# A hybrid RWKV-7 and Mamba-2 layer: gram results and chain outputs kept twice, block matrices in 64 columns, values and normed outputs transposed on TensorE

## The chip, the cores and the metric

The kernel runs on one core of a Trainium2 chip. The metric is the device time of one execution in microseconds (us). Before the change the median of three runs is 2758.5 us (2756.22 to 2762.81). On a difference of less than about 0.2% (5.5 us) a measurement of this kernel can't tell a change from none.

## What is computed

One inference step of a single layer over 592 rows (16 meta rows, 512 prompt rows, 64 rows of a running stream), model width 2048, all in float32. The part that matters here is the RWKV-7 mixer: 16 heads of width 64, a state matrix per head, and for every time step

```
def step(S, inp):
    r_t, w_t, k_t, v_t, kk_t, ka_t = inp
    sa = jnp.einsum('bhij,bhj->bhi', S, kk_t)
    S = S * w_t[:, :, None, :] - sa[..., None] * ka_t[:, :, None, :] + v_t[..., None] * k_t[:, :, None, :]
    return S, jnp.einsum('bhij,bhj->bhi', S, r_t)
```

Its output is normed over each head (mean and variance of 64 values), scaled and shifted by `lnx_w` and `lnx_b`; a bonus term `sum(r*k*r_k)*v` is added, and the sum is multiplied by a gate. The rest of the layer: a norm and a combined input projection ahead of the mixers, a Mamba-2 mixer beside RWKV, the output projection, a gated feed-forward net, a last norm.

## The kernel before

The whole layer is one instruction stream per engine. TensorE (PE) does the big products with float32 split into a high and a low part (three fp32r matmuls for one). These products are the main stream: input tiles `k0 r0 k1 r1 v0 k2 r2 ...` of the projection (96 matmuls of 296 columns each; `k`, `r`, `v` of eight head pairs, four `z` tiles in between), then the Mamba tiles `B C x`, the rest of `z`, the output projection (`mwo`) and the feed-forward net (`a x r y`). All else is written as generators (`go(...)`, line 206) that put their instructions into the gaps of the main stream. The order on each engine is fixed when the program is built, by a planner with a cost table (`tick` and `Timed`, lines 136 to 185): `beat` (215) looks, between groups of main matmuls, which generators are due by these costs, and lets them emit up to their next `yield`. On the chip each engine then runs its list strictly in order. Nearly every instruction of the kernel is recorded under line 159, the line of the wrapper, so groups are told apart by tile names and shapes.

RWKV runs per head pair j (two heads in the two halves of the 128 partitions), 640 padded time steps as 10 chunks of 64. Per pair:

- `shift_k`, `shift_r`, `shift_v` (708 to 723) take the projected tiles out of PSUM, `decay` and `pre_k` (725, 743) make decays and keys. `shift_v(j)` needs `vd` of pair j-1, `shift_r(j)` needs `rk` of j-1.
- `pre_r` (789) builds `KB` and `ST`, then waits at line 810 until the three `px` products of pair j-1 are emitted, and then issues 20 gram matmuls (tile `gr`, contraction over 64 partitions) in six groups. `gram_out` (770) takes each group out: masked halves to `ST` and `GB` on VectorE (DVE), blocks of the triangular system to `NX` and `NS` on ScalarE (ACT).
- Then `V.transpose(NN, NX)` (line 830), again after `px` of j-1 because `NN` shares memory with `YB`, and the triangular solve: 31 steps of two GpSimd (POOL) instructions (832 to 837).
- `steps` (855) transposes `KB` on PE (tile `tr`). `solved` (880) lays the solution out as block matrices `Zd` (two 64x64 blocks in 128 columns), makes `pm` from `NS`, and `MB` from it. `applied` (918) makes `pb = Zd^T GB` (mark `py`) and `px = MB^T pb`, ten 128x128 matmuls each, and `PT` from them.
- `values` (959) lays the values out in time order: eight DVE transposes in blocks of 32x32 into `V0`, after `cl` (chain finished) of pair j-1.
- `chain` (984) runs the ten chunks one after the other (tile `p`, two matmuls, evictions on ACT and DVE, two matmuls, a state update per chunk) and writes `Y`. It waits for the mark `chain` of j-1, which `post` of j-1 sets after it has read `Y` for the last time.
- `post` (1034) norms `Y`, transposes it back with eight DVE transposes into `yb` (mark `chain`, 1061), loads the gate into `rs` and applies `lnx_w`, `lnx_b`, bonus and gate; two DMAs write the result out.

For 64-row by 64-row work the profile's `gr` form reads 64*128 (rows x columns of the array); every other of these matmuls has the whole array, 128*128. A plain float32 matmul is two `MATMUL` records, a PE transpose one. Four PSUM banks serve the main stream, three go round among all these tasks (`get`, `put`), one is the chain's.

Of the kernel before, what the change touches and what calls it, by code (L numbers as in the profile page):

```python
# [11 lines left out]
F32R = mybir.dt.float32r  # L12
# [5 lines left out]
P = 128  # L18
# [68 lines left out]
def tile_hybrid(ctx, tc, xt, wq, wg, wd, lrw, cst, vec, s0w, s0m, y_out, sh_out, wkv_out, cv_out, sm_out):  # L87
# [61 lines left out]
    class Timed:  # L149
# [5 lines left out]
        def __getattr__(self, op):  # L155
            f, e = getattr(self.eng, op), self.e

            def call(out, *a, **k):
                r = f(out, *a, **k)  # L159
                part = 0.1 * (out.shape[0] <= 64)  # L160
                if e == "PE":
                    n = out.free_size()
                    tick(e, n / 2400 + 0.0133 if a[1].dtype == F32R else 0.175 if op == "transpose" else max(0.218, 0.15 + n / 1100))
                else:
# [37 lines left out]
    def load(dst, src):  # L202
        SY.dma_start(dst, src)
        cur[0].t = max(cur[0].t, now() + 2.5)
# [466 lines left out]
    pos_zv = pos[0]  # L671
    R, ses, MVs, st_o = {}, [], [], []
    hrow = [slice(0, 64), slice(64, 128)]
    vrow = [slice(64, 128), slice(0, 64)]

    def A2():

        lrp.close()
        al2, p2 = arena(a2p.enter_context(tc.tile_pool(name="a2p", bufs=1)).tile([P, A2W], F32, name="mem2"), A2W)
        R["al2"], R["pos2"] = al2, p2  # L680
        R["KB"] = al2(1280, NC, P)
        R["GB"] = al2(1280, NC, P)
        R["NS"] = al2(640, 5, P)
        R["NX"] = al2(1024, 32, 32)
# [12 lines left out]
        R["XX"] = al2(388)  # L697
        st_o.extend(al2(64) for _ in range(2))
        G.memset(R["NX"], 0.0)
        G.memset(R["NS"], 0.0)  # L700
        G.memset(R["Zd"], 0.0)
        unit()
        G.tensor_scalar(R["MB"], cc("idn").unsqueeze(1).broadcast_to([P, NC, P]), 1.0, None, ALU.mult)
        for h in range(2):
            G.memset(PT[h][vrow[h], :, vrow[h]], 0.0)
# [64 lines left out]
    def gram_out(j, h, c0, n, b, pg):  # L770

        yield "VA"
        gb_, st, kx = R["GB"], R["ST"][j % 2][h], 64 * h
        q, m = vrow[h], cc("m3")[:, 64 - 64 * h:192 - 64 * h]
# [6 lines left out]
        A.copy(R["NX"][hi, c0:c0 + n, :], pg[hi, 0:n, hi])  # L781
        A.copy(R["NS"][lo, c0 // 2:(c0 + n) // 2, hi], pg[lo, 0:n:2, hi])
        A.copy(R["NS"][hi, c0 // 2:(c0 + n) // 2, lo], pg[lo, 1:n:2, hi])
        put(b)
# [4 lines left out]
    def pre_r(j):  # L789
# [65 lines left out]
    def steps(j):  # L855
# [4 lines left out]
        for c0, n in groups:  # L860
# [7 lines left out]
            for h in range(2):  # L868
                A.copy(R["GB"][hrow[h], c0:c0 + n, hrow[h]], pg[hrow[h], 0:n, hrow[h]])
            for h in range(2):  # L870
# [9 lines left out]
    def solved(j):  # L880
# [16 lines left out]
        for c in range(5):  # L897
            PE.matmul(pm[:, c, :], R["NS"][:, c, :], R["ZM"][:, c], start=True, stop=True)
        aside()
        for q in range(4):  # L900
            d = slice(32 * q, 32 * q + 32)
            for e, i0, i1, g in ((V, 0, 10, 3), (V, 10, 11, 2)):
                e.tensor_copy(R["Zd"][d, :, 32 * q + 3 * i0:32 * q + 3 * i0 + g * (i1 - i0)].rearrange("p c (i g) -> p c i g", g=g),
                              Zc[d, i0:i1, 0:10 * g].rearrange("p i (g c) -> p c i g", g=g))
        cur[0].aside = False
        yield "A"
        for h in range(2):
            lo, hi = slice(64 * h, 64 * h + 32), slice(64 * h + 32, 64 * h + 64)
            for par, q in enumerate((hi, lo)):
                A.activation(R["MB"][hi, par::2, lo], pm[q, :, 0:32], AF.Copy, scale=-1.0)  # L910
        put(b)
# [6 lines left out]
    def applied(j, g, c0, n):  # L918
# [24 lines left out]
    def bonus(j):  # L943
# [90 lines left out]
    def post(j):  # L1034

        Y, MV, bon = c3(R["Y"]), MVs[0], bons[j % 2]
        yield from until(("post", j - 1), then="V")
# [6 lines left out]
        yield "A"  # L1044
        A.activation(yb, R["Y"], AF.Square)
        yield "V"
# [5 lines left out]
        V.tensor_tensor(Y, Y, bc(MV[:, NC:2 * NC]), ALU.mult)  # L1052
        yield "V"
        for w in range(2):
            for h in range(2):
                for t in range(2):
                    q = vrow[h].start + 32 * t
                    V.transpose(c3(yb)[64 * h + 32 * w:64 * h + 32 * w + 32, :, 32 * t:32 * t + 32],
                                Y[q:q + 32, :, 32 * w:32 * w + 32])
                yield "V"  # L1060
# [6 lines left out]
        yield "V"  # L1067
        V.tensor_tensor(yb, yb, rs, ALU.mult)
        SY.dma_start(YAD[j][:, 0:NS], yb[:, 0:NS])
# [4 lines left out]
    for g in range(3):  # L1074
        mark(("py", -1, g))
        mark(("px", -1, g))
    for q in ("rk", "chain", "pb", "pre", "prek", "post", "kb", "T", "vd", "Tm", "cl"):
        for i in (-1, -2):
            mark((q, i))
# [1085 lines left out]
```

## Time and profile before

| | |
|---|---|
| runs (three) | 2756.22, 2758.5, 2762.81 us |
| profiled execution, its own time | 2759.71 us |
| its span, first to last instruction | 2757.6 us |
| mean granted TensorE clock | 0.974 |
| PE busy | 2646.3 us (96%) |
| DVE busy | 2187.0 us (79%) |
| ACT busy | 1405.1 us (51%) |
| POOL busy | 385.9 us (14%) |

Each engine's busy time is set against the span; a busy PE can still run at half clock, so a row's granted clock is read with it (1.00 is 2.4 GHz, 0.50 is 1.2 GHz). The idle time ahead of an instruction is told in brackets with what ended it. The RWKV stage, from the first gram matmul at about 155 us to the last chain step at about 840 us, is where the change acts; after it PE is nearly always busy.

### The profile page before, as it was taken

What the parts mean: (1) busy time and instruction counts of PE and PEld (TensorE: products, weight loads), DVE (VectorE), ACT (ScalarE), POOL (GpSimd) and SP (SyncE); (2) the same over time, 40 slices, a digit from 0 to 9 for tenths busy, and PEclk for the clock granted to TensorE, in tenths of its full rate; (3) what the DMA queues carried; (4) which work ended last, traced back from release to release, by engine and by line L of the source; (5) the groups of instructions that cost most, each with busy time, mean ns of one, the idle gap of its engine ahead of it and who ended that gap; (6) DMA issues with size and microseconds to landing.
All of it is one profiled execution on the core that took longest, in us unless ns stands there. A gap on an engine that the chain in (4) does not pass through costs nothing.

```text
span 2757.6 us, 51938 instructions
## 1 busy us (share of the span) xinstructions
PE 2646.3 (96%) x19236; PEld 2580.2 (94%) x19236; DVE 2187.0 (79%) x4216; ACT 1405.1 (51%) x3013; POOL 385.9 (14%) x673
## 2 busy tenths in 40 slices
PE   8998899989999999999999999999999989999997
PEld 7888789988998989999999999999999989999997
DVE  7675787878878675568898888889888868888885
ACT  5645565656555453454454444545444434444544
POOL 3224334443401120120000000000000000000004
PEclk9999799999999999999999999999999999999999
DMA  5421121222222344343344444444344385654623
GB/s 182 171 71 54 52 71 58 67 62 74 61 88 86 92 145 132 114 146 122 124 159 132 151 133 142 144 146 145 131 152 130 123 275 194 218 186 156 203 71 108
DMA packets 196461, 349.57 MB, mean 127 GB/s; under 512 B 26096, under 2 KB 102000, under 8 KB 196080
## 3 DMA queue, kind: packets, MB, share of 16 engines
q1 hardware_dynamic: 196208, 346.26, 39.0%
q8 instruction: 151, 2.47, 0.4%
q14 instruction: 102, 0.84, 0.1%
HBM read 281.13 MB, written 65.06 MB: 126 GB/s over the span
## 4 chain that ended last, share of the span: by engine, by line
PE 79%; DVE 5%; ACT 5%; POOL 3%; issue 2%; DMA 2%; DVEq 0%; SPq 0%; ACTq 0%; POOLq 0%
PE y L159 15%; PE a L159 14%; PE r L159 14%; PE x L159 7%; PE mwo L159 7%; DVE mem L159 4%; POOL mem L159 3%; PE mx L159 3%; ACT mem L159 3%; PE mv L159 3%; PE mk L159 2%; PE mr L159 2%; PE mz L159 2%; PE p L159 2%; PE me L159 2%
## 5 line engine op out<-in xcount | busy, mean ns | idle before, releaser
L159 ACT CAST memr<-mem 128x512 fp32r<-128x512 f32 (+2 forms) x1230 | 714.1, 586 | 900.2 <-PE y L159 208.2
L159 DVE TENSOR_TENSOR memr<-mem,memr 128x512 fp32r<-128x512 f32 (+2 forms) x1076 | 691.8, 648 | 262.0 <-ACT memr L159 257.4
L159 DVE TENSOR_TENSOR mem<-mem 128x576 f32<-128x576 f32 (+9 forms) x1016 | 696.9, 702 | 21.7 <-DMA mem<-x1d 10.8
L159 POOL TENSOR_TENSOR mem<-mem 128x84 f32<-128x84 f32 (+28 forms) x583 | 337.0, 579 | 2218.8 <-ACT mem L159 1553.8
L159 ACT ACTIVATE mem<-mem 64x64 f32<-64x64 f32 (+12 forms) x413 | 217.1, 534 | 174.6 <-DVE mem L159 155.1
L159 PE MATMUL y<-memr 128*128 128x288 f32 x1352 | 206.6, 300 | 15.3 <-DVE mem L159 15.3
L159 PE MATMUL mwo<-memr 128*128 128x288 f32 x1536 | 210.4, 298 | 0.0
L159 PEld LDWEIGHTS mwo<-memr 128*128 128x128 f32 x1536 | 205.9, 189 | 3.0 <-issue 2.5
L159 PEld LDWEIGHTS y<-memr 128*128 128x128 f32 x1352 | 192.2, 192 | 15.9 <-issue 15.9
L159 PE MATMUL r<-ffm,memr 128*128 128x288 f32 x1348 | 202.7, 297 | 1.6 <-DMA ffm<-pd 1.1
L159 PE MATMUL x<-memr 128*128 128x288 f32 x1352 | 201.4, 295 | 0.0
L159 PE MATMUL y<-ffm,memr 128*128 128x288 f32 x1356 | 201.2, 295 | 0.2
L159 PE MATMUL a<-memr 128*128 128x288 f32 x1352 | 199.7, 294 | 1.2 <-DVE memr L159 1.2
L159 PE MATMUL r<-memr 128*128 128x288 f32 x1352 | 199.1, 294 | 0.0
L159 PE MATMUL a<-ffm,memr 128*128 128x288 f32 x1328 | 197.1, 295 | 0.0
L159 PEld LDWEIGHTS r<-ffm,memr 128*128 128x128 f32 x1348 | 188.3, 190 | 2.8 <-ACT ffm L159 1.3
L159 PEld LDWEIGHTS y<-ffm,memr 128*128 128x128 f32 x1356 | 187.7, 188 | 0.7 <-DMA ffm<-pd 0.4
L159 PEld LDWEIGHTS a<-memr 128*128 128x128 f32 x1352 | 186.9, 188 | 1.4 <-DVE memr L159 1.4
L159 PEld LDWEIGHTS x<-memr 128*128 128x128 f32 x1352 | 187.8, 188 | 0.0
L159 PEld LDWEIGHTS r<-memr 128*128 128x128 f32 x1352 | 186.2, 188 | 0.0
L159 PEld LDWEIGHTS a<-ffm,memr 128*128 128x128 f32 x1328 | 183.9, 188 | 0.0
L159 PE MATMUL mk<-memr 128*128 128x296 f32 x768 | 125.3, 313 | 4.6 <-DVE mem L159 4.6
(184 smaller groups left out, 4051.6 us busy)
## 6 DMA issues: line engine op xcount, KB each, us to landing
mem<-in_wg SPq DMA_DIRECT2D x176, 512.0 KB, 3.4
mem<-in_wq SPq DMA_DIRECT2D x268, 256.0 KB, 2.7
mem<-in_wd SPq DMA_DIRECT2D x128, 320.0 KB, 3.3
pd<-mem SPq DMA_DIRECT2D x280, 144.0 KB, 2.0
memr<-pd SPq DMA_DIRECT2D x80, 288.0 KB, 6.3
ffm<-pd SPq DMA_DIRECT2D x60, 288.0 KB, 6.6
mem<-lrd SPq DMA_DIRECT2D x16, 320.0 KB, 3.8
mem<-in_xt SPq DMA_DIRECT2D x16, 296.0 KB, 5.7
```

Source lines behind the costliest of these rows:

```text
L159: r = f(out, *a, **k)
```

## The change

Six things, in the order of the diff:

1. The planner's table prices a matmul whose stationary operand has 64 rows at 0.6 of what it had (grams too).
2. `GB`, `NS` and `Y` exist twice, by the parity of j; the second `Y` lies in `rs`. `Zd`, `MB` and `NS` have 64 columns, each half of the partitions holding its own 64x64 block.
3. `pm`, `pb` and `px` are two matmuls of 64x64 blocks each instead of one of 128x128.
4. The grams of pair j wait for the `NN` transpose of j-1 and the `pb` products of j-2, instead of the `px` products of j-1. The chain of j waits for `chain` of j-2 and `cl` of j-1.
5. `values` and `post` transpose on PE (helper `turn`: nine transposes of 128 columns, one half one, and one small matmul that turns chunk 0 into the other half), and evict with ACT copies (values, seven) or with DVE `tensor_scalar` (post, seven), which also apply `lnx_w` and `lnx_b`.
6. The gate is loaded into `bon`, after the bonus was added, instead of into `rs`.

```diff
-  tick(e, ... else max(0.218, 0.15 + n / 1100))
+  tick(e, ... else max(0.218, 0.15 + n / 1100) * (0.6 if a[0].shape[0] == 64 else 1))
...
-        R["GB"] = al2(1280, NC, P)
-        R["NS"] = al2(640, 5, P)
+        R["GB"] = [al2(1280, NC, P)]
+        R["NS"] = [al2(320, 5, 64) for _ in range(2)]
...
-        R["Y"] = al2(TR)
+        Ys.extend((al2(TR), rs))
...
-        R["Zd"], R["MB"] = al2(1280, NC, P), al2(1280, NC, P)
+        R["GB"].append(al2(1280, NC, P))
+        R["Zd"], R["MB"] = al2(640, NC, 64), al2(640, NC, 64)
...
-        yield from until(*[("px", j - 1, g) for g in range(3)], then="P")
+        yield from until(("nt", j - 1), *[("py", j - 2, g) for g in range(3)], then="P")
...
         V.transpose(NN, NX.rearrange("p c t -> p t c"))
+        mark(("nt", j))
...
-            PE.matmul(pm[:, c, :], R["NS"][:, c, :], R["ZM"][:, c], start=True, stop=True)
+            for q in hrow:
+                PE.matmul(pm[q, c, :], R["NS"][j % 2][q, c, :], R["ZM"][q, c], start=True, stop=True)
...
-            PE.matmul(pg[:, c - c0, :], R["Zd"][:, c, :], R["GB"][:, c, :], start=True, stop=True)
+            for q in hrow:
+                PE.matmul(pg[q, c - c0, :], R["Zd"][q, c, :], R["GB"][j % 2][q, c, :], start=True, stop=True)
...
-            PE.matmul(pg[:, c - c0, :], R["MB"][:, c, :], yb_[:, c - c0, :], start=True, stop=True)
+            for q in hrow:
+                PE.matmul(pg[q, c - c0, :], R["MB"][q, c, :], yb_[q, c - c0, :], start=True, stop=True)
...
+    def turn(dst, a, c):
+        if c < NC - 1:
+            PE.transpose(dst, a[:, CH * c:CH * c + 2 * CH], cc("idn"))
+        else:
+            PE.transpose(dst[0:64], a[:, CH * c:], cc("idn"))
+            q = hrow[0]
+            PE.matmul(dst[64:128, 0:64], a[q, 0:CH], cc("idn")[q, q], start=True, stop=True)
...
-        for w in range(2):
-            for h in range(2):
-                for t in range(2):
-                    q = vrow[h].start + 32 * t
-                    V.transpose(V0[q:q + 32, h, :, 32 * w:32 * w + 32],
-                                c3(zv)[64 * h + 32 * w:64 * h + 32 * w + 32, :, 32 * t:32 * t + 32])
-                yield "V"
+        for c0, n in groups:
+            yield "P"
+            b = yield from get()
+            pv = bank(b, f"vt{j}{c0}").rearrange("p (c x) -> p c x", x=P)
+            for c in range(c0, c0 + n):
+                turn(pv[:, c - c0, :], zv, c)
+            yield "A"
+            A.copy(V0[vrow[1], 1, c0:c0 + n, :], pv[vrow[1], 0:n, hrow[1]])
+            m = min(n, NC - 1 - c0)
+            A.copy(V0[vrow[0], 0, c0 + 1:c0 + 1 + m, :], pv[vrow[0], 0:m, hrow[0]])
+            if m < n:
+                A.copy(V0[vrow[0], 0, 0, :], pv[vrow[0], m, hrow[0]])
+            put(b)
...
-        yield from until(("chain", j - 1), ("pb", j), ("v", j), ("T", j))
-        EC, st, Y = ECs[j % 3], R["ST"][j % 2], c3(R["Y"])
+        yield from until(("chain", j - 2), ("cl", j - 1), ("pb", j), ("v", j), ("T", j))
+        EC, st, Y = ECs[j % 3], R["ST"][j % 2], c3(Ys[j % 2])
...
+            V.tensor_scalar(c3(yb)[hrow[0], c0:c0 + n, :], pv[hrow[0], 0:n, vrow[0]], *ab_(0), ALU.mult, ALU.add)
+            V.tensor_scalar(c3(yb)[hrow[1], c0 + 1:c0 + 1 + m, :], pv[hrow[1], 0:m, vrow[1]], *ab_(1), ALU.mult, ALU.add)
+            if m < n:
+                V.tensor_scalar(c3(yb)[hrow[1], 0, :], pv[hrow[1], m, vrow[1]], *ab_(1), ALU.mult, ALU.add)
...
-        load(rs, LRD[j, 2][:, 0:TR])
-        V.tensor_scalar(yb, yb, vv("lw", j), vv("lb", j), ALU.mult, ALU.add)
+        V.tensor_tensor(yb, yb, bon, ALU.add)
+        load(bon, LRD[j, 2][:, 0:TR])
         yield "V"
-        V.tensor_tensor(yb, yb, bon, ALU.add)
-        yield "V"
-        V.tensor_tensor(yb, yb, rs, ALU.mult)
+        V.tensor_tensor(yb, yb, bon, ALU.mult)
```

In `post` the eight DVE transposes give way to three groups of `turn` as in `values`, evicted by the `tensor_scalar` lines shown.

## Rows read from the trace of the kernel before

**Rows 1.** The page: span, and part 1 (busy time by engine).

```profile
span 2757.6 us, 51938 instructions
PE 2646.3 (96%) x19236; PEld 2580.2 (94%) x19236; DVE 2187.0 (79%) x4216; ACT 1405.1 (51%) x3013; POOL 385.9 (14%) x673
```

**Rows 2.** Stretches of the RWKV stage: us, busy PE, PEld, DVE, ACT, POOL, PEclk, DMA, GB/s.

```profile
155.00:240.00 85.00, 71.22 (x454) 66.98 (x453) 56.52 (x99) 40.51 (x98) 33.01 (x64) 0.88 0.22 69
...
300.00:346.00 46.00, 37.83 (x184) 31.96 (x183) 36.57 (x75) 30.93 (x82) 5.99 (x18) 0.65 0.14 47
...
405.00:420.00 15.00, 10.11 (x45) 7.71 (x45) 11.87 (x25) 11.12 (x37) 1.17 (x3) 0.66 0.22 74
...
490.00:500.00 10.00, 8.08 (x48) 7.03 (x47) 7.74 (x17) 6.61 (x21) 0.00 (x0) 0.83 0.33 87
...
563.00:582.00 19.00, 11.88 (x58) 10.15 (x58) 11.80 (x30) 14.19 (x43) 0.00 (x0) 0.64 0.20 66
...
sum 685.00, PE 636.85 PEld 597.83 DVE 525.52 ACT 403.18 POOL 239.00; mean PE 63.68 PEld 59.78 DVE 52.55 ACT 40.32 POOL 23.90
```

**Rows 3.** The same view for three stretches at half clock.

```profile
315.00:346.00 31.00, 26.12 (x94) 20.77 (x95) 22.01 (x45) 21.19 (x61) 5.24 (x16) 0.50 0.04 11
409.50:419.00 9.50, 6.19 (x25) 4.80 (x25) 7.43 (x16) 6.28 (x25) 0.32 (x1) 0.51 0.10 35
568.50:581.50 13.00, 8.98 (x38) 7.66 (x39) 8.76 (x22) 8.33 (x33) 0.00 (x0) 0.54 0.08 26
```

**Rows 4.** POOL's timeline (start, us, instruction): the second solve and the third.

```profile
267.82 31.15 POOL L159 TENSOR_TENSOR mem<-mem 128x31 f32<-128x31 f32 x62 [35.20 <-DVE mem L159]
...
339.58 32.54 POOL L159 TENSOR_TENSOR mem<-mem 128x31 f32<-128x31 f32 x62 [38.40 <-DVE mem L159]
```

**Rows 5.** PE's timeline between these solves (start, us, instruction [idle <-releaser]).

```profile
304.45 1.20 PE L159 MATMUL pm<-mem 128*128 128x33 f32 x10
...
313.77 0.85 PE L159 MATMUL px<-mem 128*128 128x128 f32 x4 [3.04 <-ACT mem L159]
314.87 4.24 PE L159 MATMUL gr<-mem 64*128 64x128 f32 x16 [0.25 <-ACT mem L159]
```

**Rows 6.** DVE's groups from 300 to 326 us (busy us, mean ns | idle).

```profile
L159 DVE STREAM_TRANSPOSE mem<-mem 32x320 f32<-32x320 f32 x14 | 7.0, 503 | 0.3
```

**Rows 7.** Groups by form, 100 to 1000 us (busy us, mean ns | idle before).

```profile
L159 DVE STREAM_TRANSPOSE mem<-mem 32x320 f32<-32x320 f32 x128 | 64.0, 500 | 2.5
...
L159 ACT COPY mem<-tr 64x256 f32<-64x256 f32 x64 | 22.3, 368 | 8.1 <-PE tr L159 5.5 <-DMA yad<-mem 1.9
...
L159 DVE TENSOR_TENSOR mem<-gr,mem 64x256 f32<-64x256 f32 x48 | 20.3, 422 | 3.4 <-PE gr L159 2.7
...
L159 PE MATMUL tr<-mem,mem 128*128 128x128 f32 x80 | 15.4, 317 | 0.0
...
L159 DVE TENSOR_SCALAR mem<-mem 128x640 f32<-128x640 f32 x16 | 9.3, 582 | 0.2
```

**Rows 8.** PE's timeline in a stretch without stalls, and at one burst of transposes.

```profile
459.75 2.16 PE L159 MATMUL mr<-memr 128*128 128x296 f32 x14
461.79 2.05 PE L159 MATMUL pb<-mem 128*128 128x128 f32 x16
463.60 0.78 PE L159 MATMUL mr<-memr 128*128 128x296 f32 x4
...
469.71 1.16 PE L159 MATMUL gr<-mem 64*128 64x128 f32 x8
470.80 0.54 PE L159 MATMUL mr<-memr 128*128 128x296 f32 x2
...
494.52 0.60 PE L159 MATMUL tr<-mem,mem 128*128 128x128 f32 x4
494.87 1.13 PE L159 MATMUL mv<-memr 128*128 128x296 f32 x4
```

**Rows 9.** DMA issues: tiles, queue, count, KB each, median us to landing.

```profile
mem<-lrd SPq DMA_DIRECT2D x16, 320.0 KB, 3.8
```

More of the change, by code (lines that the diff above doesn't have):

```diff
@@ L162, in call @@
                     n = out.free_size()
-                    tick(e, n / 2400 + 0.0133 if a[1].dtype == F32R else 0.175 if op == "transpose" else max(0.218, 0.15 + n / 1100))
+                    tick(e, n / 2400 + 0.0133 if a[1].dtype == F32R else 0.175 if op == "transpose" else max(0.218, 0.15 + n / 1100) * (0.6 if a[0].shape[0] == 64 else 1))
                 else:
@@ L671, in tile_hybrid @@
     pos_zv = pos[0]
-    R, ses, MVs, st_o = {}, [], [], []
+    R, ses, MVs, st_o, Ys = {}, [], [], [], []
     hrow = [slice(0, 64), slice(64, 128)]
@@ L699, in A2 @@
         G.memset(R["NX"], 0.0)
-        G.memset(R["NS"], 0.0)
+        for q in R["NS"]:
+            G.memset(q, 0.0)
         G.memset(R["Zd"], 0.0)
         unit()
-        G.tensor_scalar(R["MB"], cc("idn").unsqueeze(1).broadcast_to([P, NC, P]), 1.0, None, ALU.mult)
+        for q in hrow:
+            G.tensor_scalar(R["MB"][q], cc("idn")[q, q].unsqueeze(1).broadcast_to([64, NC, 64]), 1.0, None, ALU.mult)
         for h in range(2):
@@ L772, in gram_out @@
         yield "VA"
-        gb_, st, kx = R["GB"], R["ST"][j % 2][h], 64 * h
+        gb_, ns_, st, kx = R["GB"][j % 2], R["NS"][j % 2], R["ST"][j % 2][h], 64 * h
         q, m = vrow[h], cc("m3")[:, 64 - 64 * h:192 - 64 * h]
@@ L781, in gram_out @@
         A.copy(R["NX"][hi, c0:c0 + n, :], pg[hi, 0:n, hi])
-        A.copy(R["NS"][lo, c0 // 2:(c0 + n) // 2, hi], pg[lo, 0:n:2, hi])
-        A.copy(R["NS"][hi, c0 // 2:(c0 + n) // 2, lo], pg[lo, 1:n:2, hi])
+        A.copy(ns_[lo, c0 // 2:(c0 + n) // 2, 32:64], pg[lo, 0:n:2, hi])
+        A.copy(ns_[hi, c0 // 2:(c0 + n) // 2, 0:32], pg[lo, 1:n:2, hi])
         put(b)
@@ L868, in steps @@
             for h in range(2):
-                A.copy(R["GB"][hrow[h], c0:c0 + n, hrow[h]], pg[hrow[h], 0:n, hrow[h]])
+                A.copy(R["GB"][j % 2][hrow[h], c0:c0 + n, hrow[h]], pg[hrow[h], 0:n, hrow[h]])
             for h in range(2):
@@ L902, in solved @@
             for e, i0, i1, g in ((V, 0, 10, 3), (V, 10, 11, 2)):
-                e.tensor_copy(R["Zd"][d, :, 32 * q + 3 * i0:32 * q + 3 * i0 + g * (i1 - i0)].rearrange("p c (i g) -> p c i g", g=g),
+                e.tensor_copy(R["Zd"][d, :, 32 * (q % 2) + 3 * i0:32 * (q % 2) + 3 * i0 + g * (i1 - i0)].rearrange("p c (i g) -> p c i g", g=g),
                               Zc[d, i0:i1, 0:10 * g].rearrange("p i (g c) -> p c i g", g=g))
@@ L909, in solved @@
             for par, q in enumerate((hi, lo)):
-                A.activation(R["MB"][hi, par::2, lo], pm[q, :, 0:32], AF.Copy, scale=-1.0)
+                A.activation(R["MB"][hi, par::2, 0:32], pm[q, :, 0:32], AF.Copy, scale=-1.0)
         put(b)
@@ L933, in applied @@
         for c in range(c0, c0 + n):
-            PE.matmul(pg[:, c - c0, :], R["MB"][:, c, :], yb_[:, c - c0, :], start=True, stop=True)
+            for q in hrow:
+                PE.matmul(pg[q, c - c0, :], R["MB"][q, c, :], yb_[q, c - c0, :], start=True, stop=True)
         mark(("px", j, g))
@@ L1034, in post @@
     def post(j):
-        Y, MV, bon = c3(R["Y"]), MVs[0], bons[j % 2]
+        Y, MV, bon = c3(Ys[j % 2]), MVs[0], bons[j % 2]
         yield from until(("post", j - 1), then="V")
@@ L1044, in post @@
         yield "A"
-        A.activation(yb, R["Y"], AF.Square)
+        A.activation(yb, Ys[j % 2], AF.Square)
         yield "V"
@@ L1052, in post @@
         V.tensor_tensor(Y, Y, bc(MV[:, NC:2 * NC]), ALU.mult)
-        yield "V"
[L1054 to L1060, printed above, removed]
+        for c0, n in groups:
+            yield "P"
+            b = yield from get()
+            pv = bank(b, f"yt{j}{c0}").rearrange("p (c x) -> p c x", x=P)
+            for c in range(c0, c0 + n):
+                turn(pv[:, c - c0, :], Ys[j % 2], c)
+            yield "V"
+            m = min(n, NC - 1 - c0)
+            ab_ = lambda h: (VE[hrow[h], _VOFF["lw"][0] + j:_VOFF["lw"][0] + j + 1], VE[hrow[h], _VOFF["lb"][0] + j:_VOFF["lb"][0] + j + 1])
+            V.tensor_scalar(c3(yb)[hrow[0], c0:c0 + n, :], pv[hrow[0], 0:n, vrow[0]], *ab_(0), ALU.mult, ALU.add)
+            V.tensor_scalar(c3(yb)[hrow[1], c0 + 1:c0 + 1 + m, :], pv[hrow[1], 0:m, vrow[1]], *ab_(1), ALU.mult, ALU.add)
+            if m < n:
+                V.tensor_scalar(c3(yb)[hrow[1], 0, :], pv[hrow[1], m, vrow[1]], *ab_(1), ALU.mult, ALU.add)
+            put(b)
         mark(("chain", j))
         yield from until(("vd", j), then="V")
-        load(rs, LRD[j, 2][:, 0:TR])
-        V.tensor_scalar(yb, yb, vv("lw", j), vv("lb", j), ALU.mult, ALU.add)
+        V.tensor_tensor(yb, yb, bon, ALU.add)
+        load(bon, LRD[j, 2][:, 0:TR])
         yield "V"
-        V.tensor_tensor(yb, yb, bon, ALU.add)
-        yield "V"
-        V.tensor_tensor(yb, yb, rs, ALU.mult)
+        V.tensor_tensor(yb, yb, bon, ALU.mult)
         SY.dma_start(YAD[j][:, 0:NS], yb[:, 0:NS])
@@ L1075, in tile_hybrid @@
         mark(("py", -1, g))
+        mark(("py", -2, g))
         mark(("px", -1, g))
-    for q in ("rk", "chain", "pb", "pre", "prek", "post", "kb", "T", "vd", "Tm", "cl"):
+    for q in ("rk", "chain", "pb", "pre", "prek", "post", "kb", "T", "vd", "Tm", "cl", "nt"):
         for i in (-1, -2):
```

## The prediction

> **What bounds the kernel now.** I read the page first: PE is busy for 2646 of the 2757.6 us of the span, DVE for 2187 [rows 1]. The kernel is bound by PE, so a change can only win where PE stands still or runs at half clock, and it pays for every PE instruction that it adds. Then the stretches of the RWKV stage, 155 to 840 us [rows 2]: of 685 us PE is busy 636.9, so it stands for 48.1 us. That time is bunched. The first row, where the first pair has nothing to run beside it, holds 85 - 71.2 = 13.8 us. Four short rows hold 8.2 (300 to 346), 4.9 (405 to 420), 1.9 (490 to 500) and 7.1 us (563 to 582), together 22.1; the other 12.3 us are spread over the long rows between them. In three of the four short rows the clock falls to half as well [rows 3]; what is lost is the busy time by the missing share of the clock: 26.1 x 0.50 = 13.1, 6.2 x 0.49 = 3.0, 9.0 x 0.46 = 4.1, together 20.2 us. So the four stalls cost 22.1 + 20.2 = 42.3 us. That is the prize.
>
> What stalls there is a turnaround. On POOL the second solve ends at 267.8 + 31.2 = 299.0 and the third starts at 339.6 after 38.4 us of idling, released by DVE [rows 4]. On PE one sees what lies between [rows 5]: `pm` at 304.5, the last `px` at 313.8 after 3.0 us of waiting, and only then the grams of the next pair, from 314.9 at half clock. Line 810 makes them wait for `px`, since `pb` reads the only `GB`. The main stream has run as far ahead as its buffers let it. From 300 to 326 us DVE spends 7.0 us, 14 instructions, on 32x32 transposes [rows 6], queued ahead of the gram evictions.
>
> **The change part by part.**
>
> *Order and buffers (parts 2 and 4).* With `GB`, `NS` and `Y` kept twice, the grams of pair j+1 can run while pair j is being solved; in the turnaround only `pm`, `pb`, `px` and the `NN` transpose are left. From rows 4 and 5 the next solve could start some 3 us after the last `px`: about 317 instead of 339.6, so the turnaround falls from 40 to about 18 us. The chain no longer waits for the norm of the pair before. A pair then needs some 33 us of solve and 18 us of turnaround, less than the 72 us between the two solves of [rows 4]: PE itself becomes the limit between pairs. I take back nine tenths of the 42.3 us, 38; of the 13.8 us at the start 6 (there DVE, too, loses transposes); of the 12.3 us between 3. That is 47 us. Bounds: 28 (the plan's fixed order keeps a third of the stalls) and 62 (all but part of the start). What is late next is `pm` waiting for the solve, which I expect to stay in a pair or two.
>
> *Transposes (part 5).* DVE loses 16 transposes of 0.50 us a pair (128 for eight pairs) [rows 7] and one `tensor_scalar` of 0.58, and gets seven from PSUM. Nearest is the 64x256 product out of `gr` at 0.42, and no new one is larger, so at most 2.95: 8.58 - 2.95 = 5.6 us less a pair, 45 us of DVE's 525 in the stage [rows 2]. None of that counts by itself; it is part of why the stalls go. ACT gets seven copies a pair of at most 0.37 us [rows 7], 2.6 us, 21 in all, on an engine busy 403 of 685 us [rows 2]: hidden, though the weight casts for PE stand behind them; uncovered it would be those 21 us. PE gets 20 transposes and two small matmuls a pair. From one side: a burst of four takes 494.87 - 494.52 = 0.35 us until the main stream goes on [rows 8], 0.09 each, and a plain matmul (463.60 - 461.79)/8 = 0.226: 20 x 0.0875 + 0.45 = 2.2 us a pair, 18 in all. From the other: the group's busy time, 15.4 us for 80 [rows 7], is 0.19 each and counts the tail that the next matmul covers: 4.3 a pair, 34 in all. Six more bursts a pair also interrupt the main stream, so I take the middle, 26.
>
> *Halves (part 3).* 25 matmuls a pair become 50 of 64x64. The trace has none of these. Nothing excludes a gain: if two halves ran side by side at half of today's time, 25 x 0.113 x 8 = 23 us would be won. If they ran one after the other at today's price each, 25 x 0.226 x 8 = 45 us would be lost. Nearest is the gram, which has 64 rows: eight passes in 470.80 - 469.71 = 1.09 us, 0.136 a pass against 0.113 of `pb` [rows 8]. If two halves overlap and a pass costs what a gram's does, a pair of them costs 0.27 instead of 0.226: 25 x 0.047 x 8 = 9, I take 10 us. The Trainium skill (TensorEngine Tiling (Array Packing), Tiling Modes, Key Properties) says that tiles operate independently and can load and multiply in parallel; by that the halves cost nothing and the sum would be 10 us lower, 2737. No run here shows two tiles side by side. The same list says that changing the tiling mode drains TensorE, which speaks against the change; the trace agrees in so far as a gram's pass is the longer one.
>
> *Gate load (part 6).* The load used to be issued ahead of three DVE steps; now it follows the addition, and only the last multiplication stands behind it. It lands 3.8 us after its issue [rows 9]. On SP it waits for DVE's addition, and the weight loads queue behind it; there are three weight buffers, and a quarter tile of 24 matmuls lasts 24 x (461.79 - 459.75)/14 = 3.5 us [rows 8], so this is covered. On DVE the multiplication can hold the low halves of the weights behind it for some us; these are made two quarter tiles ahead, 7 us, so I take nothing; uncovered it is 8 x 3.8 = 30 us.
>
> *Planner's price (part 1) and the one-time memsets*: no instruction changes by a price, and POOL idles for 38 us ahead of a solve [rows 4]. Nothing.
>
> **Sum.** -47 + 26 + 10 = -11 us. The profiled execution took 2759.7 us (2757.6 span and 2.1 around it), 1.2 above the median of 2758.5, so the median after should be 2747.5; I say 2747.
>
> **The rivals.**
>
> A, the forecast: PE limits the stage, most stalls go, the added PE work eats three quarters of it. 2747. Chance 0.47.
>
> B: all but part of the stalls go (56 us) and the halves run side by side for nothing, transposes at their low price: -56 + 18 = -38, 2720. For it: a burst of transposes is short in rows 8. Against: 62 us is the most that could be won. 0.12.
>
> C, slower: the halves run one after the other, on an engine that has no slack left. -47 + 26 + 45 = +24, 2782. The place is `pm`, `pb`, `px` on PE. It decides from the point where 200 matmuls cost 47 - 26 = 21 us more, 0.105 each: a pair of halves at 0.33 us instead of 0.226. For it: a 64-row pass is already dearer than a full one. Against: halves that follow each other use other rows and columns. 0.19.
>
> D, slower: the gate load is not covered, and DVE stands for about 2.5 us a pair with the weights' low halves behind it: +20, 2767. Against: DVE is relieved at the same time. 0.08.
>
> E, it doesn't do what it says: the stalls don't come from `px` holding up the grams but from the fixed order, in which PE waits for a solve that the plan thinks done. Then only some 36 us come back, as much as is added. 2759. For it: POOL's solves vary (31.2 and 32.5 us) while the plan has one length. Against: line 810 is seen at work in [rows 5]. 0.14.
>
> **Numbers.** A counts as faster with 0.40 and, where its costs run high, as within 0.2% with 0.07; B is faster; E is within 0.2% with 0.12, else slower; C and D are slower. Faster 0.52, same 0.19, slower 0.29. 0.2%, 5.5 us, is about what a measurement can tell. The range runs from 2716 (B, a little beyond) to 2784 (C, a little beyond). Where faster holds, I expect 2730 to 2752.
>
> **What would show it.** Right: the gram rows lie inside the solve on POOL's clock; POOL's idle time between solves falls under 30 us; the half-clock stretches at about 315, 410 and 570 us are gone; PE busy in the RWKV stage rises toward 98%; 32x32 transposes are gone from DVE. Wrong: a pair of 64x64 halves takes more than 0.33 us until the next main matmul; PE waits for `pm` by several us in most pairs; DVE idles ahead of the last product of `post`, released by a DMA; the stage has few stalls and is still as long.

## The result and the profile after

The change makes the kernel slower by 0.5%: the median is 2773.01 us (four runs, 2770.97 to 2774.45) against 2760.65 for the kernel before (its runs 2756.22 to 2763.66), a ratio of 1.0052 with an interval of 1.0039 to 1.0066. Forecast were 11 us less; it became 12.4 more. The profiled execution took 2770.97 us.

The page's span and part 1 answer to [rows 1]:

```profile
span 2769.2 us, 53153 instructions
PE 2670.1 (96%) x19828; PEld 2591.3 (94%) x19828; DVE 2143.7 (77%) x4136; ACT 1423.8 (51%) x3070; POOL 378.9 (14%) x675
```

DVE lost 43.3 us, ACT gained 18.7, PE gained 23.8. The view of stretches shows where the time came from. Two rows of before, cut at the first matmul of the output projection (`mwo`, at 1009 us), then two of after, cut at the same matmul (1021 us); columns as in [rows 2]:

```profile
155.00:1009.00 854.00, 798.52 (x5555) 749.07 (x5554) 652.49 (x1425) 483.79 (x1225) 263.65 (x532) 0.94 0.24 73
...
1009.00:2757.00 1748.00, 1707.67 (x12754) 1698.71 (x12752) 1432.97 (x2642) 831.94 (x1591) 73.69 (x65) 0.99 0.46 150
```

```profile
155.00:1021.00 866.00, 819.97 (x6144) 757.80 (x6143) 609.40 (x1342) 499.03 (x1280) 257.23 (x532) 0.96 0.24 72
...
1021.00:2769.00 1748.00, 1707.97 (x12757) 1698.64 (x12754) 1433.76 (x2645) 835.23 (x1593) 73.60 (x65) 0.99 0.46 150
```

Behind `mwo` nothing changed. Ahead of it PE is busy 21.4 us longer and idle 9.5 us shorter (854 - 798.5 = 55.5, now 46.0). Busy time holds half-clock time, so I split it: in every stretch with a lowered clock, busy time times the missing share of the clock is what the clock costs, and the rest is work at full clock. Idle time and the loss to the clock together are called stalls from here on. From 155 us to `mwo` that makes

| kernel | idle | lost to the clock | work at full clock |
|---|---|---|---|
| before | 55.5 | 36.2 | 762.3 |
| after | 46.0 | 26.6 | 793.4 |

So the change gave PE 31.1 us of work and won back 9.5 + 9.6 = 19.1 us of stalls: 12.0 us more. The forecast had 36 and 47. From 155 us to `mwo` both kernels have eight stretches at half clock, together 96 us before and 65 after. Those of after that answer to [rows 3] are shorter but for one (each row is a window laid around the stretch):

```profile
322.00:331.00 9.00, 7.38 (x39) 6.31 (x38) 6.55 (x18) 6.61 (x21) 0.00 (x0) 0.81 0.22 67
...
391.00:419.00 28.00, 20.77 (x90) 15.46 (x87) 13.23 (x28) 14.75 (x40) 13.13 (x33) 0.51 0.08 24
...
497.00:504.00 7.00, 6.37 (x26) 5.95 (x27) 4.71 (x14) 4.62 (x14) 0.00 (x0) 0.52 0.29 103
...
555.00:562.00 7.00, 7.00 (x45) 6.61 (x45) 5.24 (x14) 6.81 (x15) 0.00 (x0) 0.52 0.29 96
```

The stall of [rows 5] at 315 us is nearly gone; one of 28 us at half clock stands at 391.

**The turnaround did not get shorter.** POOL's solves (timeline; start, us) answer to [rows 4]; these are the third to the fifth:

```profile
332.70 35.06 POOL L159 TENSOR_TENSOR mem<-mem 128x31 f32<-128x31 f32 x62 [51.59 <-DVE mem L159]
403.36 32.64 POOL L159 TENSOR_TENSOR mem<-mem 128x31 f32<-128x31 f32 x62 [33.55 <-DVE mem L159]
509.54 38.66 POOL L159 TENSOR_TENSOR mem<-mem 128x31 f32<-128x31 f32 x62 [68.65 <-DVE mem L159]
```

POOL idles 21 to 69 us ahead of a solve; forecast was under 30. From the second solve to the eighth that is 290 us in all, against 283 before. How long depends on where the grams start (us):

| solve | 2 | 3 | 4 | 5 | 6 | 7 | 8 |
|---|---|---|---|---|---|---|---|
| before: idle ahead of it | 35 | 38 | 41 | 46 | 47 | 40 | 35 |
| after: idle ahead of it | 21 | 52 | 34 | 69 | 32 | 50 | 32 |
| after: first gram, from the end of the last `px` | -42 | +2 | -23 | +14 | -41 | +4 | -18 |

Two bursts of grams (solves 2 and 6) start inside the solve before, as forecast; two (4 and 8) amid `pb` and `px`; three (3, 5 and 7) only behind the last `px`. The three lose what the four win. PE's timeline around the fourth solve shows one of the four:

```profile
359.93 0.63 PE L159 MATMUL p<-mem 128*128 128x64 f32 x4 [0.18 <-DVE mem L159]
...
370.29 1.17 PE L159 MATMUL pm<-mem 64*64 64x33 f32 x20
376.76 1.96 PE L159 MATMUL pb<-mem 64*64 64x128 f32 x32
378.65 1.16 PE L159 MATMUL gr<-mem 64*128 64x128 f32 x8
380.21 1.16 PE L159 MATMUL gr<-mem 64*128 64x128 f32 x8
...
386.26 1.09 PE L159 MATMUL px<-mem 64*64 64x128 f32 x16
388.23 1.16 PE L159 MATMUL gr<-mem 64*128 64x128 f32 x8 [0.41 <-ACT mem L159]
390.43 1.40 PE L159 MATMUL px<-mem 64*64 64x128 f32 x16 [1.04 <-ACT mem L159]
...
394.17 1.12 PE L159 MATMUL pb<-mem 64*64 64x128 f32 x8
396.50 1.22 PE L159 MATMUL gr<-mem 64*128 64x128 f32 x4 [1.22 <-ACT mem L159]
397.65 1.12 PE L159 MATMUL yt<-mem 128*128 128x128 f32 x4
400.06 1.12 PE L159 MATMUL px<-mem 64*64 64x128 f32 x8 [1.29 <-DVE mem L159]
```

Here the grams start before the last `px`, but 11 us after the solve (332.7 to 367.8), and 18 us after the end of the last chain step `p` of two pairs before, which is the row at 359.9. Line 801 of `pre_r` (804 in after) waits for that chain (`cl` of j-2), because `ST` exists only twice; DVE then makes four products into `ST`, and the grams follow. In the six pairs that have such a chain before them the grams start 16 to 22 us after its end. In before it was so as well: the chain ended here

```profile
292.74 0.63 PE L159 MATMUL p<-mem 128*128 128x64 f32 x4 [0.17 <-DVE mem L159]
```

and the grams of [rows 5] came at 314.9, 22 us later; for the other pairs it is 22 to 26 us. In all six pairs of before the fourth product ends within 3 us of the last `px`: two waits ended together, and the change took one of them away. That the chain is what holds the products is not shown. They start 8 us or more after it, behind other work in DVE's fixed list; ahead of the fourth solve that is the transposition of the solution of the pair before, for which DVE stands until the solve ends:

```profile
367.79 0.55 DVE L159 STREAM_TRANSPOSE mem<-mem 128x352 f32<-128x352 f32 x1 [2.07 <-POOL mem L159]
...
368.83 0.81 DVE L159 TENSOR_TENSOR mem<-mem 64x640 f32<-64x640 f32 x1
```

The second row is the first of the four products. In this order these grams could not lie inside the solve, chain or not. From the first gram to the start of the solve it takes 23 to 44 us (mean 35), before 20 to 39 (mean 28); what draws it out is not shown. A third `ST` would take the wait for the chain away; it wasn't tried.

**What was added** was priced about right. Groups by form, 100 to 1000 us, answer to [rows 7]:

```profile
L159 DVE TENSOR_SCALAR mem<-yt,mem 64x256 f32<-64x256 f32 x32 | 17.4, 545 | 5.3 <-PE yt L159 4.8
...
L159 PE MATMUL vt<-mem 128*128 128x128 f32 x72 | 11.9, 273 | 0.3 <-ACT mem L159 0.3
...
L159 ACT COPY mem<-vt 64x256 f32<-64x256 f32 x32 | 11.8, 368 | 4.7 <-PE vt L159 4.2
```

An eviction of `yt` takes 0.545 us where I had at most 0.42; DVE's total fell by 43.3 us all the same, 45 being forecast. The 32x32 transposes are gone. And PE's timeline in a stretch without stalls answers to [rows 8]:

```profile
444.08 0.77 PE L159 MATMUL pm<-mem 64*64 64x33 f32 x20
444.78 0.55 PE L159 MATMUL mk<-memr 128*128 128x296 f32 x2
...
447.06 1.96 PE L159 MATMUL pb<-mem 64*64 64x128 f32 x32
448.95 0.82 PE L159 MATMUL mk<-memr 128*128 128x296 f32 x4
...
455.37 0.60 PE L159 MATMUL vt<-mem 128*128 128x128 f32 x4
455.72 1.89 PE L159 MATMUL mk<-memr 128*128 128x296 f32 x12
```

A float32 matmul is two records, so eight pairs of halves take 448.95 - 447.06 = 1.89 us, 0.236 a pair; a whole `pb` took 0.226 [rows 8]. The halves run side by side: in the trace's single records the two halves of this burst start 6 to 7 ns apart, and one such pair follows the other by 0.109 us, where whole matmuls of [rows 8] follow each other by 0.112. `pm` got shorter: 0.70 us for five pairs of halves. A burst of four transposes takes 0.35 us, as [rows 8] had it.

### The profile page after: what moved, and what is told of

Same layout as the page of the kernel before. It is cut to its first block, busy times and chain, and to the rows that moved or that the text cites. A ratio compares the mean times of both kernels' runs of the same rounds, so it can differ in the third digit from the quotient of the medians.

```text
span 2769.2 us, 53153 instructions
## 1 busy us (share of the span) xinstructions
PE 2670.1 (96%) x19828; PEld 2591.3 (94%) x19828; DVE 2143.7 (77%) x4136; ACT 1423.8 (51%) x3070; POOL 378.9 (14%) x675
## 3 DMA queue, kind: packets, MB, share of 16 engines
q1 hardware_dynamic: 196208, 346.26, 38.5%
## 4 chain that ended last, share of the span: by engine, by line
PE 79%; DVE 5%; POOL 4%; ACT 3%; issue 2%; DMA 2%; SPq 0%; DVEq 0%; ACTq 0%; POOLq 0%
PE y L159 14%; PE a L159 14%; PE r L159 14%; PE x L159 7%; PE mwo L159 6%; DVE mem L159 4%; POOL mem L159 4%; PE mx L159 3%; PE mz L159 3%; PE mv L159 2%; PE mk L159 2%; ACT mem L159 2%; PE p L159 2%; PE mr L159 2%; PE me L159 2%
## 5 line engine op out<-in xcount | busy, mean ns | idle before, releaser
L159 DVE TENSOR_TENSOR mem<-mem 128x1024 f32<-128x1024 f32 (+9 forms) x1008 | 691.5, 702 | 28.7 <-DMA mem<-x1d 10.8
L159 POOL TENSOR_TENSOR mem<-mem 128x84 f32<-128x84 f32 (+28 forms) x583 | 330.0, 567 | 2220.3 <-ACT mem L159 1554.8
L159 ACT ACTIVATE mem<-mem 64x64 f32<-64x64 f32 (+13 forms) x413 | 216.7, 533 | 169.8 <-DVE mem L159 152.7
```

## The experiments

Five theories stood against each other. **Theory 1**: PE's added work, the transposes above all, is the loss. **Theory 2**: the new order itself (grams amid `pb` and `px`) is the loss. **Theory 3**: the transposes lengthen the chain from `post` over the bonus to the `r` tiles. **Theory 4**: the order that the planner writes is chance, worth some 10 us either way, and the price line moved it. **Theory 5**, put up ahead of experiment 9: what is won back comes from transposes leaving DVE. Ratios are to before. Stalls and work at full clock are those from 155 us to `mwo`, as in the table above (stalls 91.7 before, 72.6 after).

**1. Transposes back on DVE.** `after`, with the eight DVE transposes of `values` and of `post` as they were:

```diff
-                turn(pv[:, c - c0, :], zv, c)
...
+                    V.transpose(V0[q:q + 32, h, :, 32 * w:32 * w + 32],
+                                c3(zv)[64 * h + 32 * w:64 * h + 32 * w + 32, :, 32 * t:32 * t + 32])
```

> The changed kernel with values and normed outputs transposed on DVE again, as before the change; buffers, order and halves stay changed. Theory 1 (the PE work of the transposes, estimated at 26 us, is the loss, and the new order brings back some 20 us of stalls): PE busy falls by about 26 us, and the time lies 15 to 25 us under the changed kernel, ratio to before 0.996 to 1.000. Theory 2 (the new order itself is the loss: grams now run into pb and px of the pair before): the time stays at 1.003 or above. Theory 3 (the transposes on PE lengthen the chain of waits through post, bonus and the r tiles): 1.000 or below too, but POOL's idle time between solves gets shorter than after the change, which theory 1 doesn't ask for.

Measured 1.0075 (1.0062 to 1.0087), 2782.3 us. PE's work at full clock is 767.1, 26.3 less than in after: that is what the transposes cost PE. Yet the kernel is slower, as theory 2 had it, since the stalls rise to 110.9. Theory 1 can't stand alone, and 3 falls as the main cause.

**2. Grams wait for `px` again.** `after`, with

```diff
-        yield from until(("nt", j - 1), *[("py", j - 2, g) for g in range(3)], then="P")
+        yield from until(*[("px", j - 1, g) for g in range(3)], then="P")
```

> The changed kernel with one line undone: the grams of a pair wait for the px products of the pair before again. Theory 1: the early grams brought back stalls, so without them the time rises by 5 to 20 us over the changed kernel (ratio to before 1.007 to 1.012). Theory 2: the early grams only collide with pb and px and are held by the cl wait of two pairs before anyway, so the time is the same or falls (ratio 0.998 to 1.005), and the uneven spacing of the solves becomes even.

Measured 1.0041 (1.0029 to 1.0054): as fast as after, whose interval it overlaps. In this order the early grams win nothing, and don't lose either; theory 2 had this too.

**3. Halves alone.** `before`, with `NS`, `Zd` and `MB` in 64 columns, 25 matmuls a pair as 50, planned at 0.6:

```diff
-            PE.matmul(pg[:, c - c0, :], R["Zd"][:, c, :], R["GB"][:, c, :], start=True, stop=True)
+            for q in hrow:
+                PE.matmul(pg[q, c - c0, :], R["Zd"][q, c, :], R["GB"][q, c, :], start=True, stop=True)
```

> The kernel before with the 64-column block matrices and the doubled pm, pb and px matmuls alone (and their price in the plan). By the changed kernel's trace a pair of halves takes about 0.25 us in pb and px against 0.22, and 0.15 against 0.21 in pm: 20 x 0.03 x 8 - 5 x 0.06 x 8 = about +3 us, so same, ratio 0.999 to 1.002. If the halves cost 10 us as predicted, 1.003 to 1.004. If they are the loss, 1.005.

Measured 1.0135 (1.0118 to 1.0152), 37 us slower and outside all that was expected. But PE's work is only 5.6 us up (767.9); the stalls went from 91.7 to 120.1. The order on all engines had changed with the price.

**4. Grams at their old price.** `after`, with the 0.6 for 64x64 alone:

```diff
-... max(0.218, 0.15 + n / 1100) * (0.6 if a[0].shape[0] == 64 else 1))
+... max(0.218, 0.15 + n / 1100) * (0.6 if tuple(a[0].shape) == (64, 64) else 1))
```

> The changed kernel with the planner's factor of 0.6 kept to 64x64 blocks, so that grams (64 rows, 128 columns) have their old price again. No instruction is changed, only the order that the plan writes. Theories 1 to 3: within 5 us of the changed kernel, ratio to before 1.003 to 1.007. If the plan's too low price of grams is what spoils the order (PE has 20 grams a pair at 0.27 us that are planned at 0.16): 1.000 or below.

Measured 1.0013 (1.0004 to 1.0021), 2764.8 us: no instruction is added or removed, and 11 us of the loss go, a little short of the 1.000 or below that a spoilt order would have given back. Stalls fall to 54.3:

```profile
155.00:1006.00 851.00, 811.33 (x6146) 750.86 (x6145) 608.11 (x1343) 499.56 (x1281) 261.87 (x532) 0.98 0.24 72
```

A gram is planned at 0.27 x 0.6 = 0.16 us by the new price and takes 2 x 0.136 = 0.27 [rows 8]: 20 a pair put the planner 2.2 us early in each pair.

**5. Only the price line, on `before`.**

```diff
-... max(0.218, 0.15 + n / 1100))
+... max(0.218, 0.15 + n / 1100) * (0.6 if a[0].shape[0] == 64 else 1))
```

> The kernel before with the one planner line of the change: 64-row matmuls (the grams) priced at 0.6. Every instruction is the same, only their order differs. If the order that the plan writes is worth ten microseconds either way, as theory 4 has it, the ratio to before lies outside 0.998 to 1.002; since the grams' time is then planned too low by 2 us a pair, rather above: 1.002 to 1.010. If prices matter only where instructions change: 0.998 to 1.002.

Measured 1.0025 (1.0015 to 1.0036), stalls 101.5: 7 us slower with before's own instructions, as theory 4 had it.

**6. Halves in before's own order.** `before`, with halves on the old block matrices, each half planned at 0.5; each engine's list is that of before, with the 25 matmuls a pair doubled (DVE, ACT and POOL run the same instructions in the same order in both traces):

```diff
+                PE.matmul(pg[q, c - c0, :], R["Zd"][q, c, q], R["GB"][q, c, :], start=True, stop=True)
```

> The kernel before with pm, pb and px in halves, on the old block matrices and each half at half the plan's price: on every engine the order is that of before, instruction by instruction, only those 25 matmuls a pair are doubled. If the halves themselves cost what their bursts show (a pair of halves 0.25 us for 0.22 in pb and px, 0.15 for 0.21 in pm: about +3 us), the ratio to before is 0.999 to 1.003, and the 37 us of the experiment with the halves alone came from the new order that its prices made the plan write. If the halves are the loss, it is 1.010 or more here too.

Measured 1.0012 (1.0003 to 1.0021), work 766.1, stalls 94.9. So the halves cost PE 3.9 us, and the other 33 us of experiment 3 are its order:

```profile
155.00:1016.00 861.00, 805.77 (x5954) 747.82 (x5954) 651.67 (x1424) 483.08 (x1224) 263.22 (x532) 0.94 0.24 72
```

```profile
155.00:1043.00 888.00, 821.29 (x5960) 762.22 (x5958) 654.05 (x1423) 481.83 (x1224) 259.46 (x532) 0.93 0.23 70
```

The first row is experiment 6, the second 3: within six records of the same PE work, and 27 us more until `mwo`; the rest lies behind it (see experiment 8).

**7. Another price for PE transposes, on `before`**, to see what a shaken order does there:

```diff
-... else 0.175 if op == "transpose" else max(0.218, 0.15 + n / 1100))
+... else 0.19 if op == "transpose" else max(0.218, 0.15 + n / 1100))
```

> The kernel before with PE transposes priced at 0.19 us instead of 0.175 in the plan, 0.15 us in all of a pair's ten: a change of price that means nothing, with every instruction the same in another order. Theory 4 (the order is a matter of chance within ten microseconds): outside 0.998 to 1.002, on either side. Otherwise within it.

Measured 0.9994 (0.9985 to 1.0004): nothing, where theory 4 had a difference.

**8. `after` with prices near the measured ones**: grams as of old, halves at 0.5.

```diff
-... * (0.6 if a[0].shape[0] == 64 else 1))
+... * (0.5 if tuple(a[0].shape) == (64, 64) else 1))
```

> The changed kernel with the old price for grams and 0.5 instead of 0.6 for 64x64 halves, which is nearer to what their bursts take. With the old gram price alone the ratio to before was 1.0013. Theory 4: it moves from there by more than 3 us on either side, ratio outside 1.000 to 1.003. Otherwise 1.000 to 1.003.

Measured 1.0001 (0.9992 to 1.0010), stalls 53.2, work 795.8. Theory 4 had it outside 1.000 to 1.003; it lies just inside. With these prices the change breaks even: some 33 us are given and 38 taken back until `mwo`, which starts 5 us earlier than in before. Behind it 8 us are lost again, for PE waits there for the Mamba mixer (`yd`) and its clock falls. The rows are the stage and the 100 us behind it in experiment 8, the latter in before, and the wait:

```profile
155.00:1004.00 849.00, 810.57 (x6145) 750.57 (x6146) 605.85 (x1344) 501.28 (x1281) 259.12 (x532) 0.98 0.24 73
1004.00:1104.00 100.00, 94.49 (x670) 90.91 (x669) 58.73 (x124) 41.31 (x63) 9.55 (x8) 0.95 0.45 133
...
1009.00:1109.00 100.00, 99.65 (x733) 96.17 (x732) 60.99 (x128) 42.79 (x65) 9.67 (x8) 1.00 0.46 135
...
1012.41 3.22 PE L159 MATMUL yd<-mem 112*112 112x64 f32 x16 [3.90 <-DVE mem L159]
```

Experiments 3, 4, 11, 13, 14 and 17 take 5 to 8 us longer than before behind `mwo` too, so their ratios hold more than the RWKV stage. The turnaround is no shorter here either: POOL idles 275 us ahead of the second to eighth solve (two of them shown), and still the stalls are 38 us less.

```profile
326.11 34.58 POOL L159 TENSOR_TENSOR mem<-mem 128x31 f32<-128x31 f32 x62 [47.68 <-DVE mem L159]
...
409.23 34.56 POOL L159 TENSOR_TENSOR mem<-mem 128x31 f32<-128x31 f32 x62 [45.44 <-DVE mem L159]
```

**9 and 10. Experiment 8, with one part undone**: the wait for `px` as in 2 (the first diff), and the transposes on DVE as in 1 (the second).

```diff
-        yield from until(("nt", j - 1), *[("py", j - 2, g) for g in range(3)], then="P")
+        yield from until(*[("px", j - 1, g) for g in range(3)], then="P")
```

```diff
-                turn(pv[:, c - c0, :], Ys[j % 2], c)
...
+                    V.transpose(c3(yb)[64 * h + 32 * w:64 * h + 32 * w + 32, :, 32 * t:32 * t + 32],
+                                Y[q:q + 32, :, 32 * w:32 * w + 32])
```

> The changed kernel with the prices of the last experiment (grams as before, halves at 0.5), and the grams waiting for px of the pair before again. Theory 5 (what the change wins back comes from the transposes that left DVE; early grams win nothing, since the wait for cl of two pairs before ends as late as px): ratio 0.998 to 1.002, as with the same prices and early grams (1.0001). If early grams do win back stalls, it is slower than that: 1.004 to 1.010.

> The changed kernel with the same prices, and values and normed outputs transposed on DVE again: the buffers, the new order and the halves without the new transposes. PE has some 27 us less to do. Theory 5: the stalls come back, 25 to 45 us of them, so 1.000 to 1.006. If the buffers and the new order win back the stalls, PE's 27 us are a clear gain: 0.988 to 0.994.

Measured 1.0078 (1.0065 to 1.0091) and 1.0091 (1.0078 to 1.0104). Each part undone costs 20 us or more. In 9 the stalls are 86.2, and POOL idles 328 us ahead of the seven solves instead of 275; in 10 the stalls are 112, while PE has 25.8 us less to do than in 8:

```profile
155.00:1037.00 882.00, 814.05 (x5954) 753.67 (x5955) 649.96 (x1425) 484.77 (x1227) 255.79 (x532) 0.93 0.24 71
```

Theory 2 falls for this order: planned with truer prices, the early grams are worth having. Theory 1 falls with it: the transposes pay for their PE time. Theory 5 as it was put here had early grams winning nothing, and that was wrong.

**11. Transposes alone.** `before`, with `turn` in `values` and `post`, all else as it was.

```diff
-                    V.transpose(V0[q:q + 32, h, :, 32 * w:32 * w + 32],
...
+                turn(pv[:, c - c0, :], zv, c)
...
+                turn(pv[:, c - c0, :], R["Y"], c)
```

> The kernel before with the transposes on PE alone, all buffers, waits, matmuls and prices as before. Theory 5: PE gets 26 to 29 us of work and loses 25 to 40 us of idling and half clock before the output projection, ratio 0.995 to 1.002. If the stalls go only together with the buffers and the new order: 1.008 to 1.012.

Measured 1.0135 (1.0122 to 1.0148), work 786.7 (24.4 up), stalls 101.3. Alone they bring nothing back, where theory 5 had them win back 25 us or more:

```profile
155.00:1043.00 888.00, 831.38 (x5755) 779.66 (x5754) 612.29 (x1345) 496.28 (x1278) 265.55 (x532) 0.94 0.23 70
```

**12. Experiment 8 with transposes planned at 0.1**, what a burst measures.

```diff
-... else 0.175 if op == "transpose" else ...
+... else 0.1 if op == "transpose" else ...
```

> The changed kernel with grams priced as before, halves at 0.5 and PE transposes at 0.1 us instead of 0.175, which is what a burst of them takes in the trace. If prices near the measured ones give the better order: 0.996 to 1.000. If it is chance: anywhere from 0.998 to 1.008.

Measured 1.0038 (1.0026 to 1.0050), stalls 66.9: a truer price, and slower. Which order is good does not follow from one price.

**13 to 16. The same instructions, ordered anew**, to see whether 11, 10, 9 and 3 hang on their order: transposes planned at 0.1 in 11; halves at 0.6 in 10 and in 9; halves at 0.55 in 3. In this order:

```diff
-... else 0.175 if op == "transpose" else ...
+... else 0.1 if op == "transpose" else ...
```

```diff
-... * (0.5 if tuple(a[0].shape) == (64, 64) else 1))
+... * (0.6 if tuple(a[0].shape) == (64, 64) else 1))
```

```diff
-... * (0.6 if tuple(a[0].shape) == (64, 64) else 1))
+... * (0.55 if tuple(a[0].shape) == (64, 64) else 1))
```

> The kernel before with the transposes on PE alone, as in the earlier experiment (1.0135), and these priced at 0.1 us instead of 0.175, so that the plan writes another order of the same instructions. If 1.0135 was what the transposes cost without the buffers, it stays at 1.010 to 1.016. If it was the chance of one order (theory 4), it is far from it, somewhere from 0.996 to 1.008.

> The changed kernel with the transposes on DVE and grams at their old price, as in the earlier experiment (1.0091), with halves priced at 0.6 instead of 0.5: another order of the same instructions. If buffers and order without the new transposes really cost 25 us, 1.006 to 1.012; by theory 4 anywhere from 0.996 to 1.012, by more than 8 us away.

> The changed kernel with grams at their old price and waiting for px again, as in the earlier experiment (1.0078), with halves priced at 0.6 instead of 0.5. If early grams are worth 20 us, 1.005 to 1.010 again. If they are worth nothing, as the first pair of kernels with the low gram price said (1.0041 against 1.0052), 0.998 to 1.004.

> The kernel before with the halves alone, priced at 0.55; at 0.6 it was 1.0135, and with before's own order 1.0012. By theory 4 it lies anywhere from 1.000 to 1.014. If 64-column halves only do well in before's own order, near 1.0135.

Measured 1.0077 (1.0063 to 1.0092), 1.0098 (1.0083 to 1.0113), 1.0047 (1.0033 to 1.0060), 1.0089 (1.0075 to 1.0104). The order moves the same instructions by up to 16 us (11 and 13), and the halves by 33 us over 6, 16 and 3 (whose block matrices differ in width): theory 4, and larger than it said. But 10 stays where it was.

**17 and 18. Experiment 8 ordered anew**: transposes planned at 0.19 and at 0.14.

```diff
-... else 0.175 if op == "transpose" else ...
+... else 0.19 if op == "transpose" else ...
```

> The changed kernel with grams at their old price, halves at 0.5 and PE transposes at 0.19 us: a fourth order of the whole change with grams rightly priced (1.0013, 1.0001 and 1.0038 so far). By theory 5 (all parts together win back about as much as PE is given): 0.998 to 1.004, and below 1 only by the chance of the order. If the changed kernel can beat both, this or the next is where: 0.994 to 0.998.

> The same with PE transposes at 0.14 us, between the old price and the 0.09 that a burst takes: a fifth order. Theory 5: 0.998 to 1.004. The plan's own clock has the last input tile start earlier here than in any other order, 939 us against 953 for the kernel before and 947 for the change; if that clock told the time, this would be the fastest, 0.993 to 0.996.

Measured 0.9999 (0.9990 to 1.0008) and 0.9996 (0.9988 to 1.0005). The plan's own clock, by which 18 would have been the fastest of all at 0.993 to 0.996, did not tell the time. Experiment 18 until `mwo`:

```profile
155.00:1007.00 852.00, 810.86 (x6143) 753.33 (x6143) 608.13 (x1344) 497.74 (x1279) 265.72 (x532) 0.97 0.24 73
```

The change's work with the old gram price has now been run in five orders (4, 8, 12, 17, 18): 0.9996 to 1.0038, mean 1.0009. With the wait for `px` put back, two orders (9, 15) have a mean of 1.0063; with the transposes on DVE two (10, 14) have 1.0095. Compared at equal prices, the early grams are worth 21 and 9 us (9 against 8, 15 against 4) and the transposes 25 and 24 (10 against 8, 14 against 4); with the low gram price it is nothing (2 against after) and 6 (1 against after). Alone the transposes cost 21 and 37 us (13, 11), the halves 3 to 37. So what stands of theory 5 is that the parts lose alone and break even together. Why they need each other was not traced, and what the early grams gain is of the size of what an order alone can do. No version beat before by more than its interval.

## Why the prediction was wrong

*What bounds the kernel*: right. PE's work at full clock and its stalls account for the whole difference between before and after; DVE's 43 us less show nowhere by themselves.

*Transposes*: right. 26 us on PE were forecast; 24.4 (11), 26.3 (1) and 25.8 (10) were measured. Experiment 13 shows 18.2, with 35 PE records fewer than 11 ahead of `mwo`. The 26 was the middle between two readings, so that it came so near is partly luck. DVE lost 43.3 of 45 forecast, ACT got 18.7 of 21.

*Halves*: forecast 10, measured 3.9 (6) and 5.6 (3). They run side by side, and `pm` even gains; rival C is out. A pair of halves takes 0.236 us, far from its 0.33. What the Trainium skill (TensorEngine Tiling (Array Packing), Tiling Modes, Key Properties) says of tiles that work in parallel holds here: 0.236 against 0.226 is nearly nothing.

*Gate load*: nothing was forecast, and DVE's waits for it (155 to 1000 us) are small, with a bound of 30:

```profile
DVE mem L159 <- DMA mem<-lrd: 7.9, 5, 2.7
```

In before the same wait sums to 1.5 us. Rival D is out.

*Order and buffers*: **this step failed.** "I take back nine tenths of the 42.3 us", 47 with the rest; 19.1 came back, below my lower bound of 28. It rested on a turnaround that falls from 40 to about 18 us. POOL's idle time ahead of seven solves is 290 us after the change and 283 before, and it is 275 to 288 in the five orders with the old gram price: it fell by 22 us a solve in none. Two things were overlooked. First, "the next solve could start some 3 us after the last `px`" took `px` for the only late wait. I asked what was late next and named `pm`; in the trace of before the products into `ST` end within 3 us of the last `px`, behind the chain of two pairs before. Second, the grams had to find their place in fixed lists on PE and DVE, and only two bursts of seven came to lie inside a solve. Both are read from traces. No run took the wait for the chain away, and it stands in the orders that won back far more too, so by itself it does not explain the 28 us that were missing.

*Planner's price*: **this step failed too.** "No instruction changes by a price", so the term was nothing. With the old gram price the same instructions won back 37.4 us (4) and 38.5 (8), in five orders 24.8 to 43.1: nearer to my 47 than 19.1 is, and inside the bounds but for 12. That is right in size by another way than the forecast's, since the turnaround did not shorten in them. The price line costs after 11 us (4 against after) and before 7 (5), so it is the largest part of the miss that an experiment names. How much of that is the price being wrong, and how much the luck of one order, stays open: after has been run in a single order with the low price, 12's interval touches its own, and the kernels with a part undone are no slower with the low price than with the old one (2 against 9 and 15, 1 against 10 and 14).

Of the rivals E came nearest by its mechanism: the fixed order keeps the stalls. It had the cause in POOL's varying solves; what the runs show is that other planner prices, and so another order, free them. By time D (2767) and C (2782) lay nearer than E (2759), but what they were made of is out. That 2773 lies inside the stated range is owed to C, and so luck.

## What to carry to other kernels

Before taking a wait away, list for each pair when every condition of the waiting work, and of what feeds it, was met; if another one ends at the same time, the prize is at most the difference. In a kernel whose order is planned from a table of prices, a price is code: cost it by ordering anew, and don't judge one part of a change from one order, since here the same instructions lay up to 16 us apart, and nearly the same ones 33. Parts that each lose alone can break even together, so undo them from the whole as well as adding them to the old.

## What the runs showed that I had not expected

Two 64x64 float32 matmuls on opposite quarters of the array take 0.236 us together where one of 128x128 takes 0.226 (128 moving columns, bursts of eight). For 33 columns they are faster than the whole, as the same place in before and in experiment 6 (one order) shows; the first fence is before, the second experiment 6, and `pm` lasts until the next row:

```profile
380.74 1.20 PE L159 MATMUL pm<-mem 128*128 128x33 f32 x10
381.77 2.17 PE L159 MATMUL mz<-memr 128*128 128x296 f32 x14
```

```profile
380.58 0.77 PE L159 MATMUL pm<-mem 64*64 64x33 f32 x20
381.29 2.17 PE L159 MATMUL mz<-memr 128*128 128x296 f32 x14
```

1.03 us became 0.71. And the order's weight was unexpected: 3 and 6 do the same PE work within 2 us and differ by 33 us, 25 of them in stalls ahead of `mwo`.
